# An expert weight ring on attention's buffers, with four loads ahead of the embedding gate's and eight gate steps inside two expert blocks

## The chip, the cores and the metric

One core of one Trainium2 chip runs the kernel; the other cores are idle. The metric is the device time of one execution in microseconds, as the median of several runs. Engines are named as in the profile: PE is TensorE (the matrix engine), PEld its weight load, DVE is VectorE, ACT is ScalarE, POOL is GpSimd and SP is SyncE, which here only issues DMAs, in the order of its queue.

## The reference, cut to what matters

Two decoder layers over 256 tokens of width 1024, in float32. Each layer runs four token mixers, gates and merges them, projects the sum and applies a layer norm. Layer 0 then has a dense SwiGLU, layer 1 a top-2-of-8 expert SwiGLU. To both a per-layer embedding is added, gated by the residual stream:

```python
def moe_swiglu(h, w_router, b_router, w_gate, w_up, w_down):
    logits = (h @ w_router + b_router).astype(jnp.float32)
    top_v, top_i = lax.top_k(logits, TOP_K)
    top_w = jax.nn.softmax(top_v, axis=-1)
    comb = jnp.sum(jax.nn.one_hot(top_i, N_EXPERTS, dtype=jnp.float32) * top_w[..., None], axis=-2)
    out = jnp.zeros_like(h)
    for e in range(N_EXPERTS):
        out = out + comb[..., e:e + 1] * swiglu(h, w_gate[e], w_up[e], w_down[e])
    return out
...
x = layer_norm(ALPHA * x + merged @ w_out[i], ...)
f = moe_swiglu(x, ...)                                # layer 1
ple = jax.nn.sigmoid(x @ ple_gate_w[i] + ple_gate_b[i]) * (p[i] @ ple_w[i])
x = layer_norm(ALPHA * x + f + ple, ...)
```

The eight experts have 8 x 3 x 1024 x 3584 float32 weights, 352 MB, all of which are read once.

## The kernel before

Each layer has two pools of on-chip buffers, one after the other on the same bytes: "mix" (token mixers, merge, output projection; the pool of layer 1 is opened at L200) and "chan" (channel mixer, L669). A tile of a pool waits until every user of the pool before it is done.

At the end of "mix" the output projection runs (tok_proj with weights "wo", L653) and then the product of the embedding (L654 to L667), whose result goes to DRAM. In "chan" of layer 1 come, in the order of the code: the layer norm of both token halves with transposes into xth and xtl (L671 to L681); the router (moe_route, L684); moe_start, which gathers the tokens of the first expert (L1046, L1048, L1053); and the embedding gate x @ ple_gate_w, 16 steps of six matmuls (L95, L100, L103), eight for each token half, over weights "wpg" that tok_proj loads (L77) and splits into two parts on ACT and DVE (L81). tok_proj keeps back the last `keep` steps of the second half as closures. `embed` (L694) adds the bias, applies Tanh and multiplies by the embedding.

moe_run (`run`, L1176) computes the experts in blocks of 512 hidden columns, with PE's and SP's instructions in the order of the code. Six experts are "Small" (64 token slots, float32 matmuls straight from the loaded weights), two are "Big" (128 slots, weights split by L81). A block has a gate-up part, four loads of 1 MB with a quarter of the work each (L1065 for Small, L929, L930 and L933 for Big), and a down part, two loads of 1 MB (L1096 for Small), which runs one block of its kind later. The first blocks are (7,0) and (7,1), both Small, then the first Big block, then (7,2) and (7,3), and so on: 56 blocks, 336 loads. After each quarter `between()` runs one step of other work: the kept gate steps first, then the list `side`, with the transposes of the hidden layer (L1079, copy L1081) and the gathers of a coming expert (L950, L958).

The loads go through `pair` (L906): a ring of 12 buffers of 1 MB, nine "mraw" tiles of the "chan" pool and three "raw" tiles, which the other weight loads of the kernel use too. Load n takes the buffer of load n - 12 and waits for the last reader of that.

```python
raw = stile([P, 2 * D], F32, "mraw", NMR, mp) if n % (NMR + NRAW) < NMR else raw_pair()[:, :2 * D]
nc.sync.dma_start(raw, src)
...
def between():
    todo = early[0] if early[0] else side
    if todo:
        todo.pop(0)()
...
gu = cur.gate_up(pb, f, (lambda: None) if alone else between)
while early[0]:
    between()
while early[1]:
    early[1].pop(0)()
```

Here early[0] holds two kept gate steps and early[1] the two calls of embed, so both run in block 0. PSUM has two tiles of two banks, "sc", used by the gate sums (psg) and later by the down sums; `Banks.banks` (L1158) takes both at its first use.

Of the kernel before, what the change touches and what calls it, by code (L numbers as in the profile page):

```python
# [7 lines left out]
F32 = mybir.dt.float32  # L8
# [8 lines left out]
P = 128  # L17
S = 256
NT = S // P
D = 1024  # L20
KD = D // P
# [4 lines left out]
HP = P // 2  # L26
# [15 lines left out]
def build(ctx, tc, d):  # L42
    nc = tc.nc
# [4 lines left out]
    NRAW, NWS, NGT, NZA = 3, 4, 16, 16  # L48
# [59 lines left out]
    def tok_proj(pss, n, wsrc, act, lag, keep=0):  # L108

        ws, kept = {}, []  # L110
        for k0 in range(n + lag):
            for t in range(NT):
                k = k0 - t * lag
                if not 0 <= k < n:
                    continue
                if k not in ws:
                    ws[k] = wsplit(wsrc(k), 1024)

                def step(k=k, t=t):
                    a, sl = act(k, t)  # L120
                    mm3(*[(pss[t][:, c * 512:(c + 1) * 512], a, ws[k], sl, cs(c * 512, 512), k == 0, k == n - 1, "b")
                          for c in range(2)])

                if t == NT - 1 and k >= n - keep:
                    kept.append(step)
                else:
                    step()
        return kept
# [44 lines left out]
    with tc.tile_pool(name="psa", bufs=1, space=PSUM) as pa:  # L173
# [25 lines left out]
        for i in range(DEPTH):  # L199
            with tc.tile_pool(name=f"mix{i}", bufs=1) as mp:  # L200

# [466 lines left out]

            with tc.tile_pool(name=f"chan{i}", bufs=1) as mp:  # L669

# [12 lines left out]
                if i % 2 == 1:  # L683
                    route = moe_route(tc, d, stile, mm_ps, x_tok, xt_h, xt_l, split_into, mm3, ident, ones_bf)  # L684
                    moe_start, moe_run = moe(tc, d, mp, stile, route, split_into, raw_pair, (NRAW, NWS), ident)
                    moe_start(mm_ps)


                psg = [sc_ps() for _ in range(NT)]
                kept = tok_proj(psg, KD, lambda k: d["wpg"][i, k],  # L690
                                lambda k, t: ((xt_h, xt_l), (slice(None), t, k)), 2, 2 if i % 2 else 0)
                res, pb, kept = [], [], (kept, [])

# [16 lines left out]
                for t in range(NT):  # L710
                    if i % 2:
                        kept[1].append(lambda t=t: embed(t))
                    else:
                        embed(t)
# [180 lines left out]

def moe(tc, d, mp, stile, r, split_into, raw_pair, bufs, ident):

# [3 lines left out]
    slots, x = r["slots"], r["x"]  # L901
    NRAW, NWS = bufs
    NMR = 9
    count = [0]

    def pair(src):  # L906

        n = count[0]
        count[0] += 1
        raw = stile([P, 2 * D], F32, "mraw", NMR, mp) if n % (NMR + NRAW) < NMR else raw_pair()[:, :2 * D]  # L910
        nc.sync.dma_start(raw, src)
        return raw[:, :D], raw[:, D:]

# [107 lines left out]


    hidden = [stile([P, 512], F32, f"hsm{n}", 1, mp) for n in range(2)]
    scatters = [stile([P, 2, S], F32, f"pts{n}", 1, mp) for n in range(2)]
    made_small = [0]

    class Small:
# [3 lines left out]
        def __init__(self, bank, src, rk, wcol):  # L1031
            self.src, self.wcol, self.bank = src, wcol, bank
            self.pm = stile([P, NT, P], F32, "pm", 1, mp)
            for t in range(NT):
                v.tensor_scalar(self.pm[:, t], slots[1], rk(t), None, ALU.is_equal)
            self.xe = stile([P, KD, HP], F32, "xes", 2, mp)
            self.turn = 0
            self.pt = scatters[made_small[0] % 2]
            made_small[0] += 1
            self.steps = [lambda q=q: self.gather(q) for q in range(2)] + [self.scatter_matrix]  # L1040
# [112 lines left out]
    class Banks:  # L1153
        def __init__(self, one, other, two):
            self.gu, self.two, self.held = one, two, None
            self.pair, self.turn = (other, lambda: self.banks()[1][:, 512:]), 1

        def banks(self):  # L1158
            if self.held is None:
                self.held = self.two(), self.two()  # L1160
            return self.held

        @property
        def dn(self):
            a = self.banks()[0]
            return a[:, :512], a[:, 512:]

        @property
        def dns(self):
            return self.banks()[1][:, :512]  # L1170

# [4 lines left out]
    def run(banks, early, acc, final_rows, residual):  # L1176
# [8 lines left out]
        def between():  # L1185
            todo = early[0] if early[0] else side
            if todo:
                todo.pop(0)()

        with tc.manual_schedule(engines={mybir.EngineType.PE, mybir.EngineType.SP}):  # L1190
            made = {smalls[0]: first[0]}
            waiting = {Big: None, Small: None}
            for n, (i, f) in enumerate(blocks):
# [11 lines left out]
                gu = cur.gate_up(pb, f, (lambda: None) if alone else between)  # L1205
                while early[0]:
                    between()
                while early[1]:
                    early[1].pop(0)()
                if coming is not None:  # L1210
# [177 lines left out]
```

## Time and profile before

| | us |
|---|---|
| median of 3 runs | 1824.48 |
| lowest and highest run | 1824.36, 1825.55 |
| the profiled execution | 1825.18 |
| its span in the profile | 1823.5 |
| PE busy | 1736.4 (95%) |
| DVE busy | 902.4 (49%) |
| ACT busy | 729.8 (40%) |

The profile was taken on one execution. All times in its rows count from the start of its span. A matmul's end is modelled, so a busy PE is not PE at its peak. A wait is shown in brackets behind an instruction: the idle time before it on its engine, and what ended that. "DMA share" is the mean busy share of the core's 16 DMA engines. PE's granted clock is at its full level (1.00 in the rows by stages) all through the stretch that matters here.

### The profile page before, as it was taken

How to read it: one execution, taken by the hardware profiler on the slowest of the kernel's cores; microseconds unless marked ns; L12 is line 12 of the kernel's file. 1: busy time of each engine (PE TensorE's matmuls, PEld its weight loads, DVE VectorE, ACT ScalarE, POOL GpSimd, SP SyncE). 2: the span in 40 equal slices, each digit the busy share in tenths (PEclk: the TensorE clock that was granted, in tenths of full speed). 3: DMA queues.
4: the chain of work that ended last, by engine and by line, in shares of the span. 5: the costliest groups of instructions: out<-in, count | busy, mean ns of one | idle time of the engine just before them, and what ended most of it. 6: DMA issues, size and time to landing. Idle time of an engine off the chain costs nothing. (4 is left out here: it accounts for less than half of the span.)

```text
span 1823.5 us, 28068 instructions
## 1 busy us (share of the span) xinstructions
PE 1736.4 (95%) x11089; PEld 1269.6 (70%) x11089; DVE 902.4 (49%) x1527; ACT 729.8 (40%) x1163; POOL 78.1 (4%) x115
## 2 busy tenths in 40 slices
PE   8999999999999999999999999999999998999995
PEld 8998899889998989889975544544444553444441
DVE  6566665775556557575675333434224432133322
ACT  4445755454443454565533322333313332133310
POOL 2000012100002000001210000000000000000000
PEclk9999999999999999999999999999999999999998
DMA  7445355566553533535569999999999999999994
GB/s 260 156 146 186 105 182 185 207 229 237 189 187 122 181 121 139 202 100 180 199 236 414 401 421 421 421 421 421 421 421 421 421 421 421 421 420 421 421 421 199
DMA packets 100668, 524.10 MB, mean 287 GB/s; under 512 B 11824, under 2 KB 14640, under 8 KB 57520
## 3 DMA queue, kind: packets, MB, share of 16 engines
q1 hardware_dynamic: 98224, 520.12, 72.6%
q10 hardware_dynamic: 2304, 2.10, 0.3%
q8 instruction: 89, 1.46, 0.3%
q14 instruction: 51, 0.42, 0.1%
HBM read 519.03 MB, written 3.15 MB: 286 GB/s over the span
## 5 line engine op out<-in xcount | busy, mean ns | idle before, releaser
L81 DVE TENSOR_TENSOR wl<-raw,wh 128x1024 fp32r<-128x1024 f32 (+3 forms) x303 | 370.7, 1227 | 169.3 <-ACT wh L81 128.5
L81 ACT CAST wh<-raw 128x1024 fp32r<-128x1024 f32 (+3 forms) x303 | 306.4, 1017 | 281.7 <-PE mm L97 187.5
L95 PE MATMUL mm<-xth,wh 128*128 128x256 f32 x1472 | 363.1, 284 | 7.9 <-ACT wh L81 7.5
L97 PE MATMUL mm<-xtl,wh 128*128 128x256 f32 x1472 | 361.2, 283 | 0.0
L95 PEld LDWEIGHTS mm<-xth,wh 128*128 128x128 f32 x1472 | 278.9, 189 | 13.9 <-ACT wh L81 8.2
L97 PEld LDWEIGHTS mm<-xtl,wh 128*128 128x128 f32 x1472 | 279.0, 190 | 3.5 <-issue 1.2
L103 PE MATMUL mm<-xth,wl 128*128 128x256 f32 x1472 | 210.0, 283 | 0.0
L1065 PE MATMUL mm<-mraw,xes 128*64 128x512 f32 x824 | 193.9, 600 | 11.1 <-DMA mraw<-in_mgu 8.4
L81 DVE TENSOR_TENSOR wl<-mraw,wh 128x1024 fp32r<-128x1024 f32 x140 | 163.7, 1220 | 54.3 <-ACT wh L81 53.3
L103 PEld LDWEIGHTS mm<-xth,wl 128*128 128x128 f32 x1472 | 189.0, 190 | 2.2 <-issue 2.2
L1074 DVE TENSOR_TENSOR hsm<-hsm,mm 64x512 f32<-64x512 f32 x42 | 28.5, 678 | 311.7 <-ACT hsm L1073 311.7
L1096 PE MATMUL sc<-mraw,hts 128*64 128x512 f32 x632 | 146.0, 597 | 16.8 <-DMA mraw<-in_md 6.0
L81 ACT CAST wh<-mraw 128x1024 fp32r<-128x1024 f32 x140 | 140.3, 1049 | 53.3 <-DMA mraw<-in_mgu 39.6
L1065 PEld LDWEIGHTS mm<-mraw,xes 128*64 128x64 f32 x824 | 53.6, 136 | 121.9 <-issue 94.1
L1073 ACT ACTIVATE hsm<-mm 64x512 f32<-64x512 f32 x42 | 25.0, 594 | 263.5 <-PE mm L1065 263.5
L1065 PE MATMUL mm<-raw,xes 128*64 128x512 f32 x520 | 119.5, 598 | 2.2 <-DMA raw<-in_mgu 2.2
L1096 PEld LDWEIGHTS sc<-mraw,hts 128*64 128x64 f32 x632 | 43.1, 136 | 110.8 <-issue 80.7
L929 PE MATMUL mm<-wh,xth 128*128 128x512 f32 x224 | 96.6, 431 | 11.0 <-ACT wh L81 11.0
L930 PE MATMUL mm<-wh,xtl 128*128 128x512 f32 x224 | 88.5, 395 | 0.0
L1065 PEld LDWEIGHTS mm<-raw,xes 128*64 128x64 f32 x520 | 34.8, 136 | 70.0 <-issue 62.0
L533 POOL TENSOR_TENSOR x<-x,gt 128x256 f32<-128x256 f32 x48 | 50.0, 1064 | 601.7 <-DVE gt L531 601.7
L933 PE MATMUL mm<-wl,xth 128*128 128x512 f32 x224 | 71.3, 399 | 0.5
(347 smaller groups left out, 2293.4 us busy)
## 6 DMA issues: line engine op xcount, KB each, us to landing
mraw<-in_mgu SPq DMA_DIRECT2D x145, 1024.0 KB, 19.8
mraw<-in_md SPq DMA_DIRECT2D x107, 1024.0 KB, 19.8
raw<-in_mgu SPq DMA_DIRECT2D x79, 1024.0 KB, 19.8
raw<-in_wz SPq DMA_DIRECT2D x75, 512.0 KB, 4.1
raw<-in_wmg SPq DMA_DIRECT2D x64, 512.0 KB, 4.3
raw<-in_wv SPq DMA_DIRECT2D x24, 520.0 KB, 4.5
raw<-in_wbr SPq DMA_DIRECT2D x32, 384.0 KB, 3.6
raw<-in_fg SPq DMA_DIRECT2D x22, 512.0 KB, 4.4
```

The lines of the kernel that those rows point to most:

```text
L81: return sc.copy(hi, src), v.tensor_tensor(lo, src, hi.bitcast(F32), ALU.subtract)
L95: te.matmul(ps, ah[asl], bh[bsl], start=first, stop=False)
L97: te.matmul(ps, ah[asl], bl[bsl], start=False, stop=False)
L103: te.matmul(ps, lhs, rhs, start=False, stop=last)
L533: gp.tensor_tensor(merged[j], merged[j], gs[j], ALU.add)
L929: mm(ps, ah[asl], bh[bsl], start=first, stop=False)
L930: mm(ps, al[asl], bh[bsl], start=False, stop=False)
L933: mm(ps, lhs, rhs, start=False, stop=last_)
L1065: mm(ps[HP * s:HP * s + HP], self.xe[:, k], w[s][cols(a * 512, 512)], start=(k == 0), stop=(k == KD - 1))
L1073: sc.activation(h[:HP], ps[HP:], AF.Silu)
L1074: v.tensor_tensor(h[:HP], h[:HP], ps[:HP], ALU.mult)
L1096: mm(self.dn[HP * c:HP * c + HP], ht[:, a], w[cols(c * 512, 512)], start=(n == 0), stop=(n == 4 * NFB - 1))
```

## The change

A class `Ring` takes the place of `pair`. It is made at the start of the "chan" pool of layer 1, ahead of the layer norm. It asks first for five "mlow" tiles, then for the small tiles that start and run use (hsm, pts, xes, pm), and then for "mraw" tiles, now four. Both pools wait by tile (`reuse_waits="tile"`): a tile waits for the users of earlier tiles on its own bytes alone. Four expert loads are issued at once, behind the loads traced so far on SP; the loads of the embedding gate are issued after them. At the start of `run` five more loads are issued (4 to 7 of gate-up and the first down load). The ring has 12 buffers as before: loads 0 to 3 in mraw, 4 to 8 in mlow, 9 to 11 in raw. tok_proj keeps the last four steps of each half; those of the first half run in block 0, followed by its embed, those of the second in block 1. The banks for large and small sums are taken one by one.

```diff
     def tok_proj(pss, n, wsrc, act, lag, keep=0):
-        ws, kept = {}, []
+        ws, kept = {}, [[] for _ in range(NT)]
...
-                if t == NT - 1 and k >= n - keep:
-                    kept.append(step)
+                if k >= n - keep:
+                    kept[t].append(step)
...
-            with tc.tile_pool(name=f"mix{i}", bufs=1) as mp:
+            with tc.tile_pool(name=f"mix{i}", bufs=1, reuse_waits="tile") as mp:
...
-            with tc.tile_pool(name=f"chan{i}", bufs=1) as mp:
+            with tc.tile_pool(name=f"chan{i}", bufs=1, reuse_waits="tile") as mp:
+                if i % 2 == 1:
+                    ring = Ring(tc, mp, stile, raw_pair)
+                    ring.ahead([d["mgu"][0, n] for n in range(4)], True)
...
-                kept = tok_proj(psg, KD, lambda k: d["wpg"][i, k],
-                                lambda k, t: ((xt_h, xt_l), (slice(None), t, k)), 2, 2 if i % 2 else 0)
-                res, pb, kept = [], [], (kept, [])
+                with ExitStack() as behind:
+                    if i % 2:
+                        behind.enter_context(tc.issue_after(ring.last.ins))
+                    kept = tok_proj(psg, KD, lambda k: d["wpg"][i, k],
+                                    lambda k, t: ((xt_h, xt_l), (slice(None), t, k)), 2, 4 if i % 2 else 0)
+                res, pb = [], []
...
                     if i % 2:
-                        kept[1].append(lambda t=t: embed(t))
+                        kept[t] = (kept[t], lambda t=t: embed(t))
...
+class Ring:
+    LOW, HIGH, NRAW = 5, 4, 3
+    def __init__(self, tc, mp, stile, raw_pair):
+        self.tc, self.nc, self.mp, self.stile, self.raw_pair = tc, tc.nc, mp, stile, raw_pair
+        self.count, self.ready = 0, []
+        self.low = [self.tile("mlow", self.LOW) for _ in range(self.LOW)]
+        self.hidden = [stile([P, 512], F32, f"hsm{n}", 1, mp) for n in range(2)]
+        self.scatters = [stile([P, 2, S], F32, f"pts{n}", 1, mp) for n in range(2)]
+        self.first = [stile([P, KD, HP], F32, "xes", 2, mp), stile([P, NT, P], F32, "pm", 1, mp)]
+    def tile(self, tag, bufs):
+        return self.stile([P, 2 * D], F32, tag, bufs, self.mp)
+    def load(self, src, pin=False):
+        n = self.count % (self.LOW + self.HIGH + self.NRAW)
+        self.count += 1
+        if n < self.HIGH:
+            raw = self.tile("mraw", self.HIGH)
+        elif n < self.HIGH + self.LOW:
+            raw = self.low.pop(0) if self.low else self.tile("mlow", self.LOW)
+        else:
+            raw = self.raw_pair()[:, :2 * D]
+        ins = self.nc.sync.dma_start(raw, src)
+        if pin:
+            self.last = self.tc.keep_in_program_order(ins)
+        return raw[:, :D], raw[:, D:]
+    def ahead(self, srcs, pin=False):
+        self.ready.extend(self.load(src, pin) for src in srcs)
+    def pair(self, src):
+        return self.ready.pop(0) if self.ready else self.load(src)
...
     class Banks:
...
-        def banks(self):
-            if self.held is None:
-                self.held = self.two(), self.two()
-            return self.held
+        def bank(self, name):
+            if name not in self.held:
+                self.held[name] = self.two()
+            return self.held[name]
...
         def between():
-            todo = early[0] if early[0] else side
+            todo = early[0][0] if early and early[0][0] else side
...
+            ring.ahead([d["mgu"][0, n] for n in range(4, 8)] + [d["md"][0, 0]])
...
-                while early[0]:
-                    between()
-                while early[1]:
-                    early[1].pop(0)()
+                if early:
+                    while early[0][0]:
+                        between()
+                    early.pop(0)[1]()
```

## Rows read from the trace of the kernel before

**Rows 1.** The page, rate of the DMA engines in 40 equal slices.
```profile
GB/s 260 156 146 186 105 182 185 207 229 237 189 187 122 181 121 139 202 100 180 199 236 414 401 421 421 421 421 421 421 421 421 421 421 421 421 420 421 421 421 199
```
**Rows 2.** Busy time by stages: length, busy us of each engine, PEclk, DMA share, GB/s.
```profile
970.00:1018.00 48.00, 46.31 (x218) 26.49 (x218) 22.24 (x26) 16.82 (x22) 0.00 (x0) 1.00 1.01 421
1018.00:1025.00 7.00, 7.00 (x34) 2.30 (x32) 0.68 (x1) 0.59 (x1) 0.00 (x0) 1.00 0.81 290
1025.00:1200.00 175.00, 173.98 (x820) 87.07 (x818) 55.56 (x59) 50.61 (x71) 0.00 (x0) 1.00 1.01 421
1200.00:1780.00 580.00, 542.37 (x2430) 267.47 (x2428) 197.83 (x211) 171.94 (x227) 0.00 (x0) 1.00 1.01 421
1780.00:1800.00 20.00, 16.20 (x72) 4.66 (x70) 1.98 (x3) 0.97 (x2) 0.00 (x0) 1.00 0.85 351
```
**Rows 3.** Timeline of the SP queue: first issue, us to the last, line, load, count.
```profile
903.14 12.66 SPq L77 DMA_DIRECT2D raw<-in_wo  x8
921.82 17.94 SPq L77 DMA_DIRECT2D raw<-in_wpg  x8
947.47 2.02 SPq L911 DMA_DIRECT2D mraw<-in_mgu  x4
...
1018.42 5.48 SPq L911 DMA_DIRECT2D mraw<-in_mgu  x4
```
**Rows 4.** The SP queue's waits, 1000 to 1030 us: total, times, longest.
```profile
SPq L911 <- PE mm L1065: 9.7, 5, 5.0
```
**Rows 5.** PE's waits, 944 to 1020 us: total, times, longest.
```profile
PE sc L100 <- DVE xtl L81: 1.4, 1, 1.4
PE sc L95 <- ACT xth L81: 1.1, 1, 1.1
PE sc L1096 <- DVE xtl L81: 0.9, 1, 0.9
PE po L958 <- DVE xtl L81: 0.5, 1, 0.5
PE po L1079 <- DVE hsm L1074: 0.3, 1, 0.3
```
**Rows 6.** Timeline of ACT, 893 to 1015 us.
```profile
906.32 0.47 ACT L518 ACTIVATE gt<-mm,bmh 128x256 f32<-128x256 f32 x1 [0.19 <-PE mm L103]
...
933.10 1.05 ACT L81 CAST wh<-raw 128x1024 fp32r<-128x1024 f32 x1 [1.70 <-PE sc L100]
...
985.69 1.28 ACT L1073 ACT_TABLE_LOAD   x1
```
**Rows 7.** Timeline of PE, 966 to 1020 us: start, length, line, operation, count.
```profile
967.79 0.48 PE L95 MATMUL sc<-wh,xth 128*128 128x512 f32 x1
...
976.33 1.94 PE L1065 MATMUL mm<-mraw,xes 128*64 128x512 f32 x8
...
983.25 5.37 PE L1065 MATMUL mm<-mraw,xes 128*64 128x512 f32 x24
...
992.44 1.94 PE L1065 MATMUL mm<-mraw,xes 128*64 128x512 f32 x8
...
995.40 1.94 PE L1065 MATMUL mm<-mraw,xes 128*64 128x512 f32 x8
...
1002.93 1.16 PE L950 MATMUL po<-pm,x 128*128 128x128 f32 x8
1003.92 0.60 PE L1079 MATMUL sc<-ident,hsm 128*128 128x128 f32 x4
1005.01 0.44 PE L958 MATMUL po<-ident,pm 128*128 128x128 f32 x2 [0.48 <-DVE xtl L81]
...
1016.45 4.08 PE L1065 MATMUL mm<-mraw,xes 128*64 128x512 f32 x18
```
**Rows 8.** Timeline of the tail: a down step right behind the copy it needs.
```profile
1800.47 1.94 PE L1096 MATMUL sc<-raw,hts 128*64 128x512 f32 x8 [0.56 <-ACT hts L1081]
```
**Rows 9.** Timeline of PE at the start of layer 1.
```profile
586.77 0.66 PE L167 MATMUL po<-ident,x 128*128 128x128 f32 x4 [2.18 <-DVE x L158]
```

More of the change, by code (lines that the diff above doesn't have):

```diff
@@ L684, in build @@
                     route = moe_route(tc, d, stile, mm_ps, x_tok, xt_h, xt_l, split_into, mm3, ident, ones_bf)
-                    moe_start, moe_run = moe(tc, d, mp, stile, route, split_into, raw_pair, (NRAW, NWS), ident)
+                    moe_start, moe_run = moe(tc, d, mp, stile, route, split_into, ring, NWS, ident)
                     moe_start(mm_ps)
                 psg = [sc_ps() for _ in range(NT)]
-                kept = tok_proj(psg, KD, lambda k: d["wpg"][i, k],
-                                lambda k, t: ((xt_h, xt_l), (slice(None), t, k)), 2, 2 if i % 2 else 0)
-                res, pb, kept = [], [], (kept, [])
+                with ExitStack() as behind:
[4 more added lines that the diff above has]
+                res, pb = [], []
                 def embed(t):
@@ L893, in moe_route, with moe @@
                 scomb=scomb)
-def moe(tc, d, mp, stile, r, split_into, raw_pair, bufs, ident):
+class Ring:
[26 more added lines that the diff above has]
+        return self.ready.pop(0) if self.ready else self.load(src)
+def moe(tc, d, mp, stile, r, split_into, ring, NWS, ident):
     nc = tc.nc
@@ L901, in moe @@
     slots, x = r["slots"], r["x"]
[L902 to L912, printed above, removed]
+    pair = ring.pair
     def wsplit(raw):
@@ L1020, in finish @@
                     (lambda c=c: half(c), *(lambda c=c, t=t: scatter(c, t) for t in range(NT)))]
-    hidden = [stile([P, 512], F32, f"hsm{n}", 1, mp) for n in range(2)]
-    scatters = [stile([P, 2, S], F32, f"pts{n}", 1, mp) for n in range(2)]
+    hidden, scatters = ring.hidden, ring.scatters
     made_small = [0]
@@ L1032, in __init__ @@
             self.src, self.wcol, self.bank = src, wcol, bank
-            self.pm = stile([P, NT, P], F32, "pm", 1, mp)
+            self.pm = ring.first.pop() if ring.first else stile([P, NT, P], F32, "pm", 1, mp)
             for t in range(NT):
                 v.tensor_scalar(self.pm[:, t], slots[1], rk(t), None, ALU.is_equal)
-            self.xe = stile([P, KD, HP], F32, "xes", 2, mp)
+            self.xe = ring.first.pop() if ring.first else stile([P, KD, HP], F32, "xes", 2, mp)
             self.turn = 0
@@ L1154, in __init__ @@
         def __init__(self, one, other, two):
-            self.gu, self.two, self.held = one, two, None
-            self.pair, self.turn = (other, lambda: self.banks()[1][:, 512:]), 1
-        def banks(self):
-            if self.held is None:
-                self.held = self.two(), self.two()
-            return self.held
+            self.gu, self.two, self.held = one, two, {}
+            self.pair, self.turn = (other, lambda: self.bank("small")[:, 512:]), 1
+        def bank(self, name):
+            if name not in self.held:
+                self.held[name] = self.two()
+            return self.held[name]
         @property
         def dn(self):
-            a = self.banks()[0]
+            a = self.bank("large")
             return a[:, :512], a[:, 512:]
@@ L1169, in dns @@
         def dns(self):
-            return self.banks()[1][:, :512]
+            return self.bank("small")[:, :512]
         def ax(self):
```

## The prediction

> **What bounds the kernel now.** I read the rate of the DMA engines over the whole span first, then the same by stages, then the SP queue's issue times and what they waited for, and last TensorE's idle time around the place that this showed. The span has two halves. Up to slice 20 the DMA engines move 100 to 260 GB/s; from slice 21 to the last but one they stand at 421 [rows 1]. In that second half they are never idle from 1025 us to about 1797 (20 us at 351 of 421 GB/s are 16.7 us) while TensorE has slack, 542 of 580 us busy; before it, from 1018 to 1025, they move only 290 [rows 2]. So the time is what 1025 to 1797 takes, plus a tail that the change does not touch, and the question is what fixes the start of that unbroken stretch.
>
> The hole at 1018 tells it. Number the expert loads in order: 0 to 3 gate-up of block 0, 4 to 7 of block 1, 8 and 9 block 0's down weights, 10 to 13 the first large block, 14 to 17 the next small one, and so on. There are 12 buffers, so load 26 goes where load 14 lay. It is issued at 1018.42 [rows 3], and SP's waits there are for L1065 on TensorE [rows 4]: the first quarter of the third small block (7,2), which starts at 1016.45 [rows 7] (the large block's 48 matmuls end there) and has to be done with load 14. From that issue, 310 of 336 loads are left: 310 x 1.0486 MB / 421 GB/s = 772 us, and 2.5 us for two rows of 0.52 MB, which gives 1793; what was missing between 1018 and 1025 and the first landing carry it to 1797. The next three follow 1.7 us apart (5.48 us for four), closer than the 2.49 us that one takes, so load 26 binds, not its successors. **The end therefore hangs on one TensorE event, the first quarter of block (7,2).** TensorE's way to it is nearly solid: from 944 to 1020 it waits 4.1 us in five places, 2.4 of these on the layer norm [rows 5].
>
> **The change, part by part.**
>
> *Four loads early.* They are pinned behind the last load of the output projection, which issues by 915.8 (903.14 + 12.66) instead of 947.47 [rows 3]. Counting tiles in the order in which the code first asks for them, the four "mraw" tiles lie on attention's masks, softmax tiles and small constants; the last reader of any of these is the gate activation with bmh, at 906.32 [rows 6]. So nothing is waited for, and 4 x 2.49 = 10 us of transfer move to about 916 to 928. Behind them on SP stand the eight embedding-gate loads, whose first two are held by "raw" buffers until 921.82 as before; 4.2 MB from 916 and two times 0.5 MB end at about 929 by their bytes, and the first is cast at 933.10 [rows 6]. That leaves 4 us for the latency of a load: cost nothing. If that cover is gone, because the early loads start 5 us later, the first gate cast is about a us late, and four casts at most follow before the layer norm, so I bound it by 1 us. Loads 4 to 8 go to the low tiles, on buffers that the output projection and the embedding product read last; the whole pool was free at 947.47, so they are issued between 945 and that, then the row and embed loads. TensorE needs load 4 at about 982, load 8 at 996. By themselves the early loads shorten nothing: load 26 still waits for the same quarter block.
>
> *Eight gate steps instead of two in the blocks.* Of 16 steps, 8 now run before block 0. Before, 8 were done when the gather of the first expert ended, and six more ran from 967.79 to 976.33, 1.42 us each [rows 7]. So block 0 begins at about 968.0 instead of 976.33. But the six steps come back inside blocks 0 and 1, before the event that counts: the work on TensorE is the same and only its seams change. Two quarters with a step each take 983.25 - 976.33, so 3.46 us a pair; three quarters alone take 5.37, so 1.79 each [rows 7]; 3.46 - 1.79 - 1.42 = 0.25 us of seam per step, **+1.5 us** for six.
>
> The four gathers of the large expert lose their places, since block 1's gaps now hold gate steps; they run in a row ahead of the large block. A quarter with a gather took 995.40 - 992.44 = 2.96, a gather with no quarter 1003.92 - 1002.93 = 0.99 [rows 7]: 0.18 of seam saved three times, **-0.5 us**.
>
> The three waits of 0.9, 0.5 and 0.3 us [rows 5] belong to the old order; **-1.7 us**. The new one has its own. Block 0's transposes now come after block 1 with nothing between them and their copy: 0.56 us, as in the tail [rows 8]. The gathers alternate between two banks, and one holds its bank from 1002.93 until the wait on its eviction ends at 1005.01, 2.08 us [rows 7]: with the order gather, transpose, gather, gather, gather, transpose and 0.99 or 0.60 us each, the second gather waits 0.5, the fourth 0.1. Sum **+1.2 us**. Together +1.5 - 0.5 - 1.7 + 1.2 = **+0.5 us**.
>
> *ScalarE's order.* The second embedding half (Tanh) now lies between two Silu's. One table load of 1.28 us stands today where Tanh gives way to Silu [rows 6]; there will be two more. ScalarE is busy 16.8 of 48 us there [rows 2], so I take nothing. The dearer question is whether the copy after block 0's transposes is queued behind that Tanh: the add ahead of it takes 1.2 us and Tanh 1.06, against 0.6 of transposes, so at most 1.8 us. I take 0, as the copy is ready first; ends 0 and +1.8. [...]
>
> *Waits by tile, not by pool.* The expert memsets on VectorE can move up to 925 to 945, into a VectorE that is full around the layer norm, where TensorE waits 1.4 us on it [rows 5]: ends -1.4 and +1.0, taken 0. At the start of layer 1 the mask building can start earlier, beside the norm that ends TensorE's 2.18 us wait [rows 9]; of it at most all can go, and a mask operation ahead of the norm's own would add about half a us: ends -2.2 and +0.5, taken 0, since the norm's own chain ends that wait. *Banks:* asking for the two banks apart frees the small one from the second embedding half; it costs nothing.
>
> **Sum:** +0.5 us, with ends of about -3 and +3.8. The profiled execution took 1825.18 us (span 1823.5), 0.7 above the median of 1824.48; a change of +0.5 on the median gives 1825.0.
>
> **Rivals.**
>
> *A, the bytes count.* DMA engines at 421 GB/s for 770 us look like the bound, and 10 us of their work now lie in idle time: 1824.5 - 10 = 1814.5. [...] For it: the rate. Against it: the hole at 1018, which shows the ring full and TensorE behind; loads that come earlier make that hole longer. At most the 2.2 us missing in it (7 us at 290 of 421) would be had without a faster TensorE. Chance 0.12.
>
> *B, the gathers in a row.* If each gather waits for the eviction of the one before (as the down step L1096 waits 0.9 us for a gather's eviction [rows 5], though it writes the other bank of that tile), four take 4 x 2.08 instead of 4 x 0.99, +4.4 us in place of the 0.6 taken: +0.5 + 3.8 = +4.3, 1828.8, slower. It decides when TensorE's idle time between block 1 and the large block passes 4.3 us. For it: that wait. Against: the gathers' two banks are different tiles. Chance 0.12.
>
> *C, the waits by tile are not granted.* Then the four early loads wait for the whole pool, are issued at 947.47 as before [rows 3], and the gate's loads stand behind them: 947.47 + 10 + 1.2 us of bytes puts the first at 958.7 without its latency. Cast and subtraction (1.05 us and about as much) and eight steps of 1.42 us put block 0 at 972.2 at the earliest instead of 968, +4.2 us; with a few us of latency, and what of the first gather does not fit beside the steps, +9. Taken at +7: 1831.5. Chance 0.05.
>
> **How the numbers follow.** A measurement of this kernel can tell about 0.2% from no change, 3.7 us. The sum as worked out has 0.71, its own range 1821.5 to 1828.3. B lies on the slower side, C too, and 0.04 of the sum's high end: slower 0.21. A and 0.01 of the low end: faster 0.13. Same 0.66. The range that holds 8 in 10 is the sum's with B: 1821 to 1829.5.
>
> **What would show it.** Right: four expert loads at about 916; the first matmul of block 0 near 968; the DMA rate below 421 between about 965 and 1015 (a load each 3.46 us instead of 2.49 is 300 GB/s); load 26 issued at 1018 to 1020; 421 GB/s from there to the end. Each gate step inside a block pairs at 3.46 us. Wrong: load 26 issued more than 3 us earlier or later, TensorE waiting for a gate weight near 947, or DMA engines that fall short of 421 after load 26.

## The result and the profile after

The changed kernel takes 1835.71 us (median of 5 runs, 1834.64 to 1835.83) against 1824.48 us before (1823.99 to 1826.91): a ratio of 1.0057 with an interval of 1.0045 to 1.0068, so some 11 us slower. The forecast was 1825.0 with a range up to 1829.5. The profiled execution has a span of 1834.1 us, 10.6 more than before's 1823.5.

The rate of the DMA engines comes first, as in [rows 1]. What is lower is slices 20 and 21, counted from 0 (186 and 351 where 236 and 414 stood); from slice 22 on, where before still had 401, the line is flat.

```profile
GB/s 258 153 147 185 104 185 184 209 230 231 187 184 119 191 126 133 193 130 175 209 186 351 420 421 421 421 420 421 420 421 421 420 421 420 421 420 421 421 421 206
```

By stages, answering [rows 2] with further stages ahead of them (length, busy us of PE, PEld, DVE, ACT, POOL, PEclk, DMA share, GB/s):

```profile
915.00:940.00 25.00, 25.00 (x111) 20.18 (x110) 17.11 (x23) 6.86 (x10) 3.95 (x5) 1.00 0.08 26
...
952.00:956.00 4.00, 0.55 (x7) 0.46 (x7) 3.21 (x23) 0.20 (x1) 0.00 (x0) 0.97 1.03 415
956.00:966.00 10.00, 9.32 (x40) 7.76 (x42) 3.54 (x27) 2.48 (x6) 0.00 (x0) 0.50 0.65 254
966.00:970.00 4.00, 4.00 (x19) 2.63 (x16) 3.93 (x4) 2.89 (x4) 0.00 (x0) 1.00 0.13 23
970.00:1018.00 48.00, 45.37 (x210) 26.41 (x209) 21.31 (x26) 16.04 (x22) 0.00 (x0) 1.00 1.01 415
1018.00:1025.00 7.00, 7.00 (x32) 5.71 (x31) 4.50 (x4) 3.08 (x3) 0.00 (x0) 1.00 1.01 420
1025.00:1200.00 175.00, 173.98 (x817) 87.42 (x818) 56.62 (x61) 51.49 (x71) 0.00 (x0) 1.00 1.01 421
```

Before 940 the DMA engines move 26 GB/s, not more than before as four early loads should have made it. From 952 to 956 TensorE works 0.55 us of 4, and behind that the granted clock is 0.50 for ten us. From 970 on the DMA engines run nearly unbroken, at 415 and then 420 GB/s: the hole that before has at 1018 (290 GB/s) is not there, and the last idle stretch ends at 970. The SP queue shows where the loads went, answering [rows 3] (first issue, us to the last, line, load, count):

```profile
901.27 12.79 SPq L77 DMA_DIRECT2D raw<-in_wo  x8
941.06 6.32 SPq L929 DMA_DIRECT2D mraw<-in_mgu  x4
949.95 19.32 SPq L77 DMA_DIRECT2D raw<-in_wpg  x8
969.31 1.99 SPq L929 DMA_DIRECT2D mlow<-in_mgu  x4
...
1028.51 2.06 SPq L929 DMA_DIRECT2D mraw<-in_mgu  x2
```

The four early loads go at 941.06 instead of about 916, the gate's loads behind them at 949.95 instead of 921.82, load 4, the first behind the gate's, at 969.31, and load 26 at 1028.51, 10.1 us later than in [rows 3]. SP's waits from 895 to 975 say for what (total, times, longest):

```profile
SPq L929 <- DMA pw_dram<-gt: 31.7, 3, 26.9
SPq L77 <- DVE wl L81: 19.5, 3, 10.5
SPq L77 <- DMA pw_dram<-gt: 8.0, 4, 2.5
```

The early loads wait not for a buffer but for the stores of the embedding product, which ScalarE issues at 939 to 944 and whose data these loads do not touch (e4 below shows that). The trace of before has a wait of SP for the same stores ahead of its own first expert loads (longest 5.7 us), which the prediction did not read. The longest wait for a split (L81), 10.5 us, is that of the gate's loads behind 950 for a "raw" buffer to come free. TensorE's waits from 944 to 1030, answering [rows 5], have grown from 4.1 to 10.4 us, most of it inside the routing:

```profile
PE mm L849 <- DVE selb L846: 3.0, 1, 3.0
PE sc L986 <- DVE xtl L81: 2.2, 2, 1.7
PE mm L95 <- ACT xth L81: 1.0, 1, 1.0
...
PE mm L1080 <- DVE pm L1069: 0.8, 1, 0.8
...
PE sc L1130 <- ACT hts L1115: 0.5, 1, 0.5
```

TensorE's timeline, answering [rows 7], has no gate step (L95 on `sc`) ahead of 966.89: the routing, the gather of the first expert (L1080) and block 0's first quarter (L1099) stand first.

```profile
955.61 0.17 PE L849 MATMUL mm<-selb,ut 128*128 128x8 bf16 x1 [3.00 <-DVE selb L846]
...
956.68 7.09 PE L1080 MATMUL mm<-pm,x 128*128 128x64 f32 x32 [0.80 <-DVE pm L1069]
...
964.12 2.84 PE L1099 MATMUL mm<-mraw,xes 128*64 128x512 f32 x8
966.89 0.50 PE L95 MATMUL sc<-wh,xth 128*128 128x512 f32 x1
```

Before, gate steps filled these gaps, up to the matmul on selb that here waits 3.0 us:

```profile
961.09 0.40 PE L100 MATMUL sc<-wh,xtl 128*128 128x512 f32 x1
961.57 0.17 PE L842 MATMUL mm<-selb,ut 128*128 128x8 bf16 x1
```

And ScalarE, answering [rows 6], casts the first gate weights at 965.00 instead of 933.10, with one table load in all:

```profile
965.00 3.89 ACT L81 CAST wh<-raw 128x1024 fp32r<-128x1024 f32 x4
...
978.90 1.28 ACT L1107 ACT_TABLE_LOAD   x1
988.47 0.59 ACT L1107 ACTIVATE hsm<-mm 64x512 f32<-64x512 f32 x1 [8.28 <-PE mm L1099]
991.30 1.06 ACT L709 ACTIVATE x<-x 128x1024 f32<-128x1024 f32 x1 [2.24 <-DVE x L708]
1002.30 0.59 ACT L1107 ACTIVATE hsm<-mm 64x512 f32<-64x512 f32 x1 [9.94 <-PE mm L1099]
```

### The profile page after: what moved, and what is told of

It reads as the page before. It is cut to its first block, busy times and chain, and to the rows that moved or that the text cites. A ratio compares the mean times of both kernels' runs of the same rounds, so it can differ in the third digit from the quotient of the medians.

```text
span 1834.1 us, 28037 instructions
## 1 busy us (share of the span) xinstructions
PE 1741.9 (95%) x11089; PEld 1272.2 (69%) x11089; DVE 903.4 (49%) x1527; ACT 729.4 (40%) x1163; POOL 78.0 (4%) x115
## 5 line engine op out<-in xcount | busy, mean ns | idle before, releaser
L81 DVE TENSOR_TENSOR wl<-raw,wh 128x1024 fp32r<-128x1024 f32 (+3 forms) x303 | 370.4, 1227 | 168.2 <-ACT wh L81 127.3
L81 ACT CAST wh<-raw 128x1024 fp32r<-128x1024 f32 (+3 forms) x303 | 306.4, 1018 | 275.3 <-PE mm L97 185.8
L95 PE MATMUL mm<-xth,wh 128*128 128x256 f32 x1472 | 363.8, 285 | 7.3 <-ACT wh L81 7.1
L95 PEld LDWEIGHTS mm<-xth,wh 128*128 128x128 f32 x1472 | 279.2, 190 | 13.6 <-ACT wh L81 8.2
L1099 PE MATMUL mm<-mlow,xes 128*64 128x512 f32 x520 | 123.3, 600 | 8.3 <-DMA mlow<-in_mgu 5.7
L1099 PE MATMUL mm<-raw,xes 128*64 128x512 f32 x520 | 119.9, 598 | 3.3 <-DMA raw<-in_mgu 3.3
L81 DVE TENSOR_TENSOR wl<-mlow,wh 128x1024 fp32r<-128x1024 f32 x80 | 92.8, 1221 | 24.5 <-ACT wh L81 24.4
L1099 PEld LDWEIGHTS mm<-mlow,xes 128*64 128x64 f32 x520 | 33.8, 136 | 81.6 <-issue 57.5
L81 ACT CAST wh<-mlow 128x1024 fp32r<-128x1024 f32 x80 | 79.5, 1050 | 23.6 <-DMA mlow<-in_mgu 14.7
L1130 PE MATMUL sc<-mraw,hts 128*64 128x512 f32 x352 | 81.2, 596 | 5.9 <-DMA mraw<-in_md 2.9
L81 DVE TENSOR_TENSOR wl<-mraw,wh 128x1024 fp32r<-128x1024 f32 x60 | 71.2, 1221 | 30.2 <-ACT wh L81 29.3
L1099 PEld LDWEIGHTS mm<-raw,xes 128*64 128x64 f32 x520 | 34.6, 136 | 71.8 <-issue 60.8
L1099 PE MATMUL mm<-mraw,xes 128*64 128x512 f32 x304 | 73.3, 608 | 2.7 <-DMA mraw<-in_mgu 2.1
```

What stands on the lines that cost most here:

```text
L81: return sc.copy(hi, src), v.tensor_tensor(lo, src, hi.bitcast(F32), ALU.subtract)
L95: te.matmul(ps, ah[asl], bh[bsl], start=first, stop=False)
L1099: mm(ps[HP * s:HP * s + HP], self.xe[:, k], w[s][cols(a * 512, 512)], start=(k == 0), stop=(k == KD - 1))
L1130: mm(self.dn[HP * c:HP * c + HP], ht[:, a], w[cols(c * 512, 512)], start=(n == 0), stop=(n == 4 * NFB - 1))
```

## The experiments

Two theories fit this trace. **Theory 1**: SP's wait for the stores makes the gate's weights late, and that is the loss. **Theory 2**: the line that puts the gate's loads behind the early ones moves all gate steps behind the routing in the fixed orders of ScalarE and TensorE; nothing fills the routing's waits, the clock falls, and the event on which load 26 hangs comes 10 us late, whenever the weights land.

**The stores left out** (e1_no_stores).

```diff
-                            sc.dma_start(pw_dram[t, c][:, n * S:(n + 1) * S], o)
...
-                        nc.sync.dma_start(pw[c], pw_dram[t, c])
+                        nc.sync.dma_start(pw[c], d["x"][t][:, c * 512:(c + 1) * 512])
```

> Left out: the embedding product of the last layers is not stored to memory; the gate reads pieces of the input x in its place, of the same size. With the eight stores gone, nothing of theirs is left for SP to wait for, so the four early expert loads should be issued at about 916 instead of 941.06, and the eight gate loads right behind them, by about 925 instead of 949.95. TensorE's program order is that of the changed kernel (all gate steps behind the routing and behind the first quarter of block 0). Theory 1 (the time is lost in SP's wait for the stores: 31.7 us ahead of the early loads and 8.0 ahead of the gate's): 1825, as before. Theory 2 (the time is lost in TensorE's order: with the gate steps behind the routing nothing fills the waits of the routing, 10.4 us from 938 to 1030 instead of 4.1, and the granted clock falls to 0.50 for some 10 us): 1834 to 1836, with waits and the low clock as in the changed kernel, load 26 at 1026 to 1029. Rival A of the prediction (the early bytes count): 1814.

Its total, 3281.59 us, does not speak on the question: with other data in layer 1 the loop over what the experts' capacities leave over runs too (1002 more matmuls of L964 behind 1830 us). Up to 1030 us the order of work is the changed kernel's, and that part can be read. SP:

```profile
912.75 1.89 SPq L928 DMA_DIRECT2D mraw<-in_mgu  x4
918.79 48.93 SPq L77 DMA_DIRECT2D raw<-in_wpg  x8
...
1027.74 2.06 SPq L928 DMA_DIRECT2D mraw<-in_mgu  x2
```

The early loads go 28 us sooner, the first gate loads 31 us, and load 26 goes at 1027.74 all the same, as does load 4 at 967.76. From 956 to 966 the clock is 0.50 again. This speaks for theory 2.

**The stores on GpSimd** (e4_gp_stores), the same question with all computed.

```diff
-                            sc.dma_start(pw_dram[t, c][:, n * S:(n + 1) * S], o)
+                            gp.dma_start(pw_dram[t, c][:, n * S:(n + 1) * S], o)
```

> The changed kernel with the eight stores of the embedding product (both layers) issued by GpSimd instead of ScalarE; all is computed. As in the run without the stores, SP should not wait for them: early expert loads at about 913, gate loads from about 919. TensorE's order is the changed kernel's (gate steps behind the routing and the first quarter of block 0). Theory 1 (the time is lost in SP's wait for the stores): 1825. Theory 2 (it is lost in TensorE's order): waits of 9 to 10.4 us from 938 to 1030, granted clock 0.50 for some 10 us from 955 on, first quarter of block 0 at 962 to 964, load 26 at 1026 to 1029, 1834 to 1836.

Measured 1833.78 us, ratio 1.0052 (1.0039 to 1.0065), not told apart from the changed kernel. SP no longer waits for a store, and its first issues are these:

```profile
911.89 1.85 SPq L929 DMA_DIRECT2D mraw<-in_mgu  x4
917.79 48.97 SPq L77 DMA_DIRECT2D raw<-in_wpg  x8
```

The stages show that 311 GB/s went through before 940, against 26:

```profile
915.00:940.00 25.00, 25.00 (x112) 20.28 (x111) 17.00 (x25) 6.53 (x11) 5.20 (x8) 1.00 0.78 311
940.00:956.00 16.00, 8.45 (x61) 6.41 (x59) 12.56 (x59) 3.02 (x8) 3.55 (x6) 0.93 0.12 43
956.00:966.00 10.00, 10.00 (x41) 7.24 (x41) 3.47 (x9) 4.99 (x8) 0.00 (x0) 0.60 0.00 0
```

It buys nothing: the casts of the gate's weights still stand in ScalarE's order behind the routing's last copy, so the rest of the gate's loads wait for buffers, SP is held for 49 us, load 4 behind them goes at 966.80, and the DMA engines are idle until then.

```profile
961.72 0.74 ACT L1090 COPY pts<-mm 64x256 f32<-64x256 f32 x2
962.49 3.90 ACT L81 CAST wh<-raw 128x1024 fp32r<-128x1024 f32 x4
```

Theory 1 falls: the wait for the stores is real, and removing it alone is worth nothing that can be measured.

**The order taken out, the early loads kept** (e5_no_behind).

```diff
-                    if i % 2:
-                        behind.enter_context(tc.issue_after(ring.last.ins))
```

> The changed kernel with its four early loads, but without the order that puts the gate's loads behind them: the eight gate loads stand ahead of the four again. TensorE's order is that of the run without early loads. Theories 1 and 2: 1825 (1823.5 to 1827): the gate's loads go at 922 as before, the four early loads behind them at about 941 to 943, some 5 us ahead of before's 947.47, which buys nothing as load 26 waits for TensorE. Rival A (bytes count): 1820, as 5 us of transfer move ahead. Rival (the early transfers themselves, or the seams, cost the time): 1830 to 1836.

Measured 1825.0 us, ratio 0.9993 (0.9984 to 1.0002): all 11 us are back. Gate steps stand between the routing's again, TensorE waits 4.2 us from 944 to 1022, the gather takes 3.23 us for 28 of its matmuls, and block 0 starts where the prediction had it:

```profile
964.45 3.23 PE L1078 MATMUL mm<-pm,x 128*128 128x64 f32 x28
...
967.84 1.94 PE L1097 MATMUL mm<-mraw,xes 128*64 128x512 f32 x8
...
971.28 1.94 PE L1097 MATMUL mm<-mraw,xes 128*64 128x512 f32 x8
...
974.74 1.94 PE L1097 MATMUL mm<-mraw,xes 128*64 128x512 f32 x8
```

**Without the early loads** (e3_no_early).

```diff
-                    ring.ahead([d["mgu"][0, n] for n in range(4)], True)
...
-                    if i % 2:
-                        behind.enter_context(tc.issue_after(ring.last.ins))
...
-            ring.ahead([d["mgu"][0, n] for n in range(4, 8)] + [d["md"][0, 0]])
+            ring.ahead([d["mgu"][0, n] for n in range(8)] + [d["md"][0, 0]])
```

> The changed kernel without the four early loads, and so without the order that puts the gate's loads behind them; all nine loads are asked for in the block loop. What stays: 8 gate steps inside two blocks, the ring's buffers, the waits by tile, the banks. TensorE's order has gate steps between the routing's steps again. Theories 1 and 2: 1825 (1823.5 to 1827), load 26 at 1018 to 1020, block 0 near 968, a granted clock of 1.00 throughout. Rival (the seams of the eight gate steps, or the gathers in a row, cost it): 1830 to 1836, with load 26 that much later. If the steps in the blocks are worth something by themselves: below 1823.

Measured 1826.08 us, ratio 0.9997 (0.9987 to 1.0006). So the 8 gate steps in two blocks, the gathers in a row and the waits by tile together cost nothing that can be measured, and the early loads of e5 gain nothing that can be.

**The pools as a whole** (e2_pool_waits).

```diff
-            with tc.tile_pool(name=f"mix{i}", bufs=1, reuse_waits="tile") as mp:
+            with tc.tile_pool(name=f"mix{i}", bufs=1) as mp:
...
-            with tc.tile_pool(name=f"chan{i}", bufs=1, reuse_waits="tile") as mp:
+            with tc.tile_pool(name=f"chan{i}", bufs=1) as mp:
```

> The changed kernel with the two pools waiting as a whole again, as before the change. Theories 1 and 2: the early loads wait anyway (for stores, until 941.06), so they move by some us at most (to 945 to 948, where the pool is free), the gate loads with them (950 to 957); theory 1 gives up to 1837, or a few us more, theory 2 stays at 1835 to 1836 unless gate weights become late for TensorE, then 1836 to 1842. If the waits by tile cost something elsewhere (the experts' memsets or the masks of the next layer ahead of a norm), it is below 1834.

Measured 1836.28 us, ratio 1.0056 (1.0042 to 1.007). The early loads go at 947.14, six us later than in the changed kernel, and the time is the same.

**Work in the routing's hole** (e8_warm), to price the clock.

```diff
     ps = mm_ps()
+    for n in range(8):
+        te.matmul(ps[:, 256:512], ident, x_tok[1][:, n % 4 * 256:n % 4 * 256 + 256], start=True, stop=True)
     te.matmul(ps[:, 0:NE], ut, selb[:, 0], start=True, stop=True)
```

> The changed kernel with 8 more matmuls (128x128 by 128x256, of the layer's x, into an unused part of a bank, never read), which stand in TensorE's order between the router's transposes and the first matmul on selb, where TensorE waits 3.00 us in the changed kernel. A 128x128 one takes 0.145 us (1.16 for eight), so these take some 2.3 to 3.5 us. Theory 2 with the clock as part of the price: the granted clock stays at 1.00 or falls later, the gather takes 3.2 to 4 us instead of 7.09 and the first quarter 1.94 instead of 2.84, so up to 4.8 us come back: 1831. If the clock falls all the same, or its fall is not what makes the gather long: 1834 to 1837.

```profile
953.94 0.29 PE L811 MATMUL mm<-ident,lt 8*128 8x8 f32 x2 [0.57 <-DVE lt L807]
954.16 3.72 PE L850 MATMUL mm<-x,ident 128*128 128x256 f32 x16
...
958.78 3.79 PE L1082 MATMUL mm<-pm,x 128*128 128x64 f32 x32 [0.80 <-DVE pm L1071]
```

The added matmuls fill the 3.0 us, the granted clock is 1.00 from 952 to 964, the gather takes 3.79 us instead of 7.09 and the first quarter 1.94 instead of 2.84: 4.2 us. From L811 to load 26 it is 1026.39 - 953.94 = 72.45 us, in the changed kernel 1028.51 - 952.32 = 76.19, so 3.7 us come back in this stage. The gate steps move with the gather (first at 964.74 instead of 966.89) and load 4 too (967.95): counted from the first load of the output projection, load 4 comes 2.7 us sooner than in the changed kernel, and the end 2.6. The time, 1834.7 us with a ratio of 1.005 (1.0037 to 1.0063), is too wide to show it by itself.

**The early loads really early** (e10_act_gate), for rival A: e5 with the gate's loads issued by ScalarE and layer 1's stores by GpSimd.

```diff
-        nc.sync.dma_start(raw[:, :cols], src)
+        (eng or nc.sync).dma_start(raw[:, :cols], src)
...
-                    ws[k] = wsplit(wsrc(k), 1024)
+                    ws[k] = wsplit(wsrc(k), 1024, sc if keep else None)
...
-                            sc.dma_start(pw_dram[t, c][:, n * S:(n + 1) * S], o)
+                            (gp if i % 2 else sc).dma_start(pw_dram[t, c][:, n * S:(n + 1) * S], o)
```

> The kernel with its early loads and without the order that puts the gate's loads behind them, with the eight gate loads issued by ScalarE and the stores by GpSimd, so that the four early loads stand right behind the output projection's on SP. They should go by about 925, some 15 to 20 us ahead of the 944.28 of the run in which they stood behind the gate's. TensorE keeps gate steps between the routing's. Theory (the end hangs on a TensorE event): 1823 to 1827, with a larger hole at 1018; the bytes buy nothing. Rival A of the prediction (the early bytes count): 1812 to 1817. If ScalarE is held up by the gate's loads waiting for buffers: the layer norm late, 1827 to 1835.

Measured 1831.38 us, ratio 1.0034 (1.0021 to 1.0047). The loads go from 923.38 on and 284 GB/s flow from 915 to 940 instead of before's 170, yet the kernel is slower. It was not a clean trial: all gate steps that are not kept for the blocks now come ahead of the routing's end, and the routing's wait stands bare once more:

```profile
963.47 0.17 PE L847 MATMUL mm<-selb,ut 128*128 128x8 bf16 x1 [2.79 <-DVE selb L844]
...
964.54 7.09 PE L1078 MATMUL mm<-pm,x 128*128 128x64 f32 x32 [0.80 <-DVE pm L1067]
```

Eight runs give one table (us; first load of the output projection, load 4, load 26, span; the last two columns are the span less the issue of load 4 and of load 26):

| kernel | first wo load | load 4 | load 26 | span | L4 to end | L26 to end |
|---|---|---|---|---|---|---|
| before | 903.14 | 954.82 | 1018.42 | 1823.5 | 868.7 | 805.1 |
| after | 901.27 | 969.31 | 1028.51 | 1834.1 | 864.8 | 805.6 |
| e2 pools as a whole | 902.63 | 970.39 | 1030.49 | 1835.9 | 865.5 | 805.4 |
| e3 no early loads | 902.03 | 947.14 | 1019.98 | 1825.2 | 878.1 | 805.2 |
| e4 stores on GpSimd | 899.08 | 966.80 | 1025.95 | 1832.0 | 865.2 | 806.1 |
| e5 order taken out | 901.39 | 946.40 | 1019.43 | 1824.1 | 877.7 | 804.7 |
| e8 work in the hole | 902.66 | 967.95 | 1026.39 | 1832.9 | 865.0 | 806.5 |
| e10 loads at 923 | 900.80 | 942.44 | 1024.80 | 1829.7 | 887.3 | 804.9 |

In before, e3, e5 and e10 the DMA engines have a hole from 1018 to 1025 (290, 231, 233 and 288 GB/s), and the end follows the issue of load 26 by 804.7 to 805.2 us. In the four kernels that keep the gate's loads behind the early ones (after, e2, e4, e8) there is no such hole: 420 or 421 GB/s. Load 26 then only joins loads that are under way, and the end follows it by 805.4 to 806.5. What these four share is SP, held by the gate's loads until it issues load 4, and the unbroken stretch that starts there: 864.8 to 865.5 us from load 4 to the end. Neither theory has this last link: the order that theory 2 names is the cause, but in these kernels it reaches the end through load 4 and not through load 26. The first column also shows that the profiled executions differ by up to 4 us before any of this begins.

**Four small blocks ahead of the first large one** (e9_lead4): e3 with one number changed, to move the event itself.

```diff
-    LEAD, TRAIL = 2, 4
+    LEAD, TRAIL = 4, 4
```

> The kernel without the four early loads, with the first large block after four small blocks instead of two (LEAD 4). In the run without early loads the DMA engines moved 396 of 421 GB/s from 966 to 1018 and 231 of 421 from 1018 to 1025: 3.1 and 3.2 us of transfer are missing, because load 26 waits for a quarter that stands behind the large block's 48 matmuls. Theory (the end hangs on when the ring's buffers come free, so on TensorE's order of blocks): the hole at 1018 goes, and up to 6.3 us with it: 1819 to 1822. Rival (the end hangs on TensorE's sum of work, or on something later): 1825 as before, with the hole at another place. If the large blocks end later for it: above 1826.

Measured 1821.02 us, ratio 0.9977 (0.9968 to 0.9985): faster than both kernels. Its stages:

```profile
915.00:940.00 25.00, 25.00 (x113) 20.34 (x113) 17.99 (x23) 11.20 (x15) 3.67 (x6) 1.00 0.50 171
940.00:966.00 26.00, 23.54 (x141) 18.65 (x140) 22.42 (x72) 9.18 (x18) 1.88 (x2) 1.00 1.00 400
966.00:1025.00 59.00, 58.54 (x278) 26.34 (x278) 14.13 (x23) 9.76 (x18) 0.00 (x0) 1.00 1.01 414
1025.00:1060.00 35.00, 35.00 (x172) 18.61 (x173) 11.21 (x12) 11.09 (x16) 0.00 (x0) 1.00 1.00 402
```

The hole at 1018 is gone but for 402 of 421 behind it.

**The same number in the kernel before** (e9_before_lead4).

```diff
-    LEAD, TRAIL = 2, 4
+    LEAD, TRAIL = 4, 4
```

> The kernel before, with the first large block after four small blocks instead of two, and nothing else. Theory: its hole from 1018 to 1025 (290 of 421 GB/s, 2.2 us) goes; block 0 still starts near 976, so the transfers before it (345 GB/s from 940 to 966 against 400) stay: 1822 to 1823.5. If the change's two blocks with 8 gate steps are worth nothing in this order of blocks: 1821, as without early loads. Rival: 1824.5.

**Three small blocks** (e9_lead3), in the kernel of e3.

```diff
-    LEAD, TRAIL = 2, 4
+    LEAD, TRAIL = 3, 4
```

> The kernel without the four early loads, with the first large block after three small blocks. With four, DMA engines moved 412 to 414 of 421 GB/s from 966 to 1100, and TensorE was busy without a gap from 1025 to 1200, so both are near their limit; with two, TensorE's quarter behind the large block was the limit. Three lies between: 1820.5 to 1823.5. Below 1820 if TensorE's gap-free stretch was costing the run with four.

Before with four gives 1821.87 us, ratio 0.9984 (0.9975 to 0.9993): most of the gain is this one number, and whether the change's blocks add to it is not told apart. Three gives 1826.51 us, ratio 1.0003 (0.9993 to 1.0012), a miss: the hole only moves, to 356 GB/s from 1025 to 1060.

**The same number in the changed kernel** (e11_after_lead4).

```diff
-    LEAD, TRAIL = 2, 4
+    LEAD, TRAIL = 4, 4
```

> The changed kernel with one number changed: the first large block after four small blocks instead of two. In the changed kernel TensorE reaches the quarter that frees load 14's buffer 10 us late. With the large block out of the way, that quarter is no longer what the end hangs on. Theory (the end hangs on the ring and so on TensorE's order; what is left of the loss is the transfers that SP issues late): up to 966 the changed kernel moved 4.75 us of transfer less than the LEAD 4 run without early loads (323 against 400 GB/s from 940), so 1821 + 4.75 = 1826, at most 1829, which takes back most of the 11 us. Rival (TensorE is behind by 10 us whatever the order of blocks, and stays behind): 1834 to 1836.

Measured 1836.67 us, ratio 1.0054 (1.004 to 1.0068): a miss by over 7 us, and by time the rival's number. The number that takes the kernel of e3 from a ratio of 0.9997 to 0.9977 gains nothing here, so load 26 is not what the end of the changed kernel hangs on. Load 4 goes at 971.70, and from it to the end it takes 864.7 us, as in the four kernels above with the other order of blocks. The stages show the bytes:

```profile
915.00:940.00 25.00, 24.24 (x111) 19.61 (x110) 17.14 (x24) 7.44 (x12) 5.16 (x7) 1.00 0.13 46
940.00:966.00 26.00, 19.34 (x108) 16.06 (x107) 17.89 (x68) 5.32 (x14) 2.40 (x3) 0.81 0.83 323
966.00:1025.00 59.00, 58.54 (x255) 29.58 (x256) 20.82 (x24) 16.24 (x22) 0.00 (x0) 0.97 0.91 372
1025.00:1060.00 35.00, 35.00 (x178) 19.74 (x176) 12.12 (x15) 11.84 (x18) 0.00 (x0) 1.00 1.02 421
```

Summed over these four stages e9_lead4 moves 53.2 MB and this kernel 46.2: 6.9 MB at 421 GB/s are 16.5 us, and the spans differ by 1836.4 - 1819.6 = 16.8. I had counted only the expert loads that came late. But the gate's eight loads (4.2 MB) went into the idle time before 940 in e9_lead4, and here they take the place of expert loads behind 950. Behind 1060 both run at 421 GB/s, so nothing is made good.

**Both** (e10_act_gate_lead4): e10_act_gate with four small blocks.

```diff
-    LEAD, TRAIL = 2, 4
+    LEAD, TRAIL = 4, 4
```

> The kernel with ScalarE issuing the gate's loads, GpSimd the stores, and the four early loads on SP from 923 on, with the first large block after four small ones. In the run with two, 284 GB/s were moved from 915 to 940 instead of 171 (6.7 us of transfer early), but the end followed load 26 and TensorE's late routing. With the large block out of the way: if bytes are now what counts (rival A under this order of blocks), 6.7 us early less 1.8 us lost from 940 to 966: 1816 to 1818. If TensorE's later block 0 (971.98 against 967.03) counts: 1825 to 1827.

Measured 1828.79 us, ratio 1.0013 (1.0004 to 1.0022), above both theories' numbers. Bytes moved early (289 GB/s from 915 to 940) do not pay there while TensorE's routing is late: block 0's first quarter runs from 972.73 to 976.41, SP issues no load from 963.85 to 976.45, and from 966 to 1025 the DMA engines move 331 GB/s.

## Why the prediction was wrong

**What bounds the kernel: right for the kernel before, not for the changed one.** Where the hole stands ahead of load 26 (before, e3, e5, e10) the end follows that load. In the changed kernel load 26 went 10.1 us later and the span grew by 10.6, which is the "wrong" sign that was named; but the DMA engines had no hole there, so its issue did not set the end. The end hangs on where the unbroken stretch starts, at load 4: the prediction had loads 4 to 8 issued between 945 and 947.47, and they went from 969.31 on, behind the gate's loads. That the two numbers agree is a near tie of the two paths: 804.7 to 805.2 us behind load 26 would be 1833.2 to 1833.7 (an estimate from the other four kernels), against a span of 1834.1. e11 moved the one and left the other, and gained nothing.

**"So nothing is waited for": the first step that failed.** The buffers were free as counted, but the loads were held by something other than their buffers. SP waited 31.7 us at the early loads for ScalarE's stores. The prediction looked for what is queued behind the new loads, and not for what they themselves are behind. With the stores on GpSimd's queue the wait is gone.

**"Cost nothing", bounded by 1 us: the step that cost the time.** It asked when the gate's first weight lands, and took the order in which TensorE and ScalarE do their work as unchanged. (The sum's high end leaves even that bound out: 0.5 + 1.8 + 1.0 + 0.5 is its 3.8.) Both orders are fixed ahead of the run (in e4 the gate's loads go 32 us sooner, at 917.79, and their casts stand behind the routing's last copy all the same, at 962.49), and the line that issues the gate's loads behind the early ones moved all gate steps, and the casts for them, behind the routing. The first cast went from 933.10 to 965.00; the casts and splits free the buffers for the rest of the gate's loads (SP waits 19.5 us for splits), and load 4 stands behind those on SP. e4 has the first weights in time and is as slow; e5 takes out that one line and is back at 1825.0. On TensorE the same line removed a cover that I had not named: gate steps stood in the routing's gaps. Worked from the traces of after and e5: 10.4 - 4.2 = 6.2 us of waits, and 4.2 us of clock (e8), 10.4 us together, where load 26 goes 9.1 us later than in e5.

**The clock was no term of the sum.** With 0.55 us of work in 4 the granted clock fell to 0.50, and the next 10 us ran at that level. e8 shows the gather at 3.79 instead of 7.09 us when the gap is filled, at a granted clock of 1.00.

**The seams: right as far as can be told.** Predicted +0.5; e3 and e5 measure ratios of 0.9997 and 0.9993. In e5 block 0 starts at 967.84 (predicted 968.0, but e5 is 1.8 us ahead of before at the first load of the output projection), a quarter and a step 3.46 us apart, one copy waited for 0.5 us (0.56). The gathers wait 2.2 us in the changed kernel where 0.6 was taken, short of rival B's 4.4.

**ScalarE's order: right in its price, wrong in its count.** The prediction took nothing for two more table loads; there were no more, so that the price held says nothing for the reason given. The prediction had one row to go by, the load of 1.28 us where Tanh gives way to Silu [rows 6]. In the changed kernel the trace has one of 1.28 us at 978.90 and none between the Silu of 988.47, the Tanh of 991.30 and the Silu of 1002.30, so the two loads that the prediction counted there did not come.

**The rivals.** C came nearest (1831.5, with loads at 947.47 and the gate's behind them) but by another cause: waits by tile were granted. e2 has C's condition, the loads at 947.14, and its ratio of 1.0056 is some 10 us where C took 7: C too left the casts in their old places. A is not borne out: in e4 and e10 the bytes went early and the kernel was slower than before. In e4 what was won ahead of 940 was lost again while SP was held (43 and 0 GB/s); in e10 TensorE was late.

What stays open: no run brings load 4 forward and leaves TensorE's order as it is, so what the change costs by each of the two paths alone is read from traces and from e11. The clock's part is shown in its stage (3.7 us) and not in the median, and an early load behind an undisturbed routing was not had, as e10 changed TensorE's order too.

## What to carry to other kernels

Here ScalarE and TensorE ran in orders that are fixed ahead, and an edit that delayed loads also moved the work that hangs on them on both engines (the first cast from 933.10 to 965.00, the first gate step from 946.69 to 966.89); ask of such an edit which gaps that work was filling, and which other loads stand behind the delayed one in its queue. When a ring is full, find the event that frees its next buffer and move that event (here one number in the order of blocks, 0.9977). See first that the DMA engines have a hole at that event: in the changed kernel they had none, and the same number gained nothing. An event that comes late by as much as the kernel does is not yet what the kernel waits for. And of a load that is to go early, look at all that it can wait for, other queues' transfers among them (here 26.9 us for ScalarE's stores), not at its buffer alone.

## What was not expected of the hardware

A load on SP waited up to 26.9 us for stores of ScalarE that share no data with it, and not at all once GpSimd issued the stores. The granted clock was at 0.50 from 956 to 966 after four us in which TensorE was busy 0.55, while the gaps of 1.1 and 1.4 us around 947 in the kernel before [rows 5] left it at 1.00; in e3, with gaps of 1.2 us at the same place, it read 0.70 from 946 to 949 and 0.73 to 952, and in e8, ahead of the added matmuls, 0.52 from 949 to 952. When a short gap lowers it is not settled here.
